# Attention scores of two heads at once on the two row halves of the array, six rounds instead of eleven steps, nine eviction buffers

## The chip, the cores and the metric

The kernel runs on one core of a Trainium2 chip, as one program. TensorE (PE, and PEld for its weight loads) multiplies, VectorE (DVE), ScalarE (ACT) and GpSimd (POOL) work on vectors, and SyncE (SP) issues the transfers from HBM. The metric is the device time of one execution in microseconds, less is better.

## The reference, cut to what matters

The program is two blocks of two layers each, on 256 tokens of width 1024, in float32. Each block has attention with 8 heads over the 256 tokens, causal and with a softmax over float32 scores. Block 1's mixer runs it beside a causal convolution over 31 tokens; block 2's mixer has three branches, of which A has 8 heads of 64 columns, B 4 heads with two score maps each, C 8 heads whose queries and keys are 64 + 32 columns.

```python
def mixer(u, cos, sin, ...):                      # block 1
    q, k, v, glu_in, g_attn, g_conv = jnp.split(u @ w_in, splits, axis=-1)
    attn = moba_attention(q, k, v)                # 8 heads of 64, causal at 256 tokens
    y_attn = attn @ w_attn_br
    y_conv = conformer_conv(glu_in, ...)          # depthwise, 31 taps, layer norm, silu, product
    merged = jax.nn.sigmoid(g_attn) * y_attn + jax.nn.sigmoid(g_conv) * y_conv
    return merged @ w_out
...
sc = jnp.einsum('brnqhc,brnkhc->brnhqk', qb, kw).astype(jnp.float32) * scale + bias   # branch A
p = probs(qa, k1) - lam * probs(qb, k2)                                               # branch B
sc = (einsum(qn, k_nope) + einsum(qr, k_rope)).astype(jnp.float32) * scale            # branch C
```

## The kernel before, in words

The main stream on PE is made of products with weights that stream in from HBM in pieces of 1 MB. Each piece is split into a high and a low part (ACT L138 writes `whi`, DVE L139 `wlo`), and `ws` (L160, L161, L164) multiplies both: 24 matmuls for one tile of 128 output columns. The attentions and the convolution are generators, "tracks", that advance beside this stream. `track(gen, steps, us)` registers one, and the stream calls `tick` after each `ws`, which takes as many steps as are due; `finish` takes all that are left, at once. So one step of an attention lies between two `ws`, and its position is fixed when the program is written.

`attend` has eleven steps. Step st issues the outputs of the pair of heads before (`matmul` L471 and L473, at odd steps from 3), the transposes of the probabilities of head st - 1 (`p_t`, three transposes at L450, then an ACT copy at L452), and the scores of head st (`probs`, L429 for the 128 queries of the first half, L430 for the others). Behind the scores DVE adds the bias and takes the negated row maximum (L433, L435), ACT takes the exponentials with row sums (L438, L439), DVE the reciprocal (L442), and `normalise` scales the numerators, the first 128 columns on ACT (L486), the others on DVE (L487). PE reads in the float32 form, which the trace shows as two instructions for each such matmul (one for each transpose). Everything that is copied out of PSUM or held for the softmax comes from the tag `ev`, 5 buffers of 2 KB a partition, used in turn.

A head of 64 columns fills 64 of the array's 128 rows: in block 1 and in branch A the heads 2i and 2i + 1 lie on the upper and the lower 64 partitions of the same tile (`qkf`). In branch C the operands are padded to 128 rows. Branch B (`diff`, L1328 to L1337) calls `probs` twice in a row, for its two maps on the two halves.

In block 1 the depthwise convolution is a track too (`conv`, L909 and L912 on DVE, 124 instructions in all). `mixer1` finishes the attention, then the convolution, and then transposes the convolution's result on PE (`conv_ln`, L927) for its layer norm. In the first layer other work on the small matmuls L408 and L418 lies between the `ws` as well, whose result DVE takes at L421.

Of the kernel before, what the change touches and what calls it, by code (L numbers as in the profile page):

```python
# [13 lines left out]
ALU = mybir.AluOpType  # L14
PSUM = bass.MemoryType.PSUM

P = 128
# [21 lines left out]
# columns of the packed per-partition parameters, and of the shape constants  # L39
# [21 lines left out]
PARTS = ((0, 512), (512, 768), (768, 1024))  # of the columns at the end of a product of 1024  # L61
# [3 lines left out]
class Net:  # L65
# [28 lines left out]
    def ev(self):  # L94
        return self.t("one", [P, 512], tag="ev", bufs=5)
# [6 lines left out]
    def track(self, gen, steps, us):  # L102
        """Advance gen by `steps` steps over the next `us` of the main stream."""
        t = [gen, steps / us, 0.0]
        self.tracks.append(t)
        return t
# [17 lines left out]
    def fetch(self, parts=1):  # L124
        """One packed piece of a weight: its float32 values as hi + lo, both float32r."""
# [16 lines left out]
    def w(self, ahead=2):  # L142
        """The next piece in weight_order; the pieces after it are already on their way."""
        while self.queue and len(self.ready) < 1 + ahead:
            self.fetch()
        return self.ready.pop(0)

    def split(self, hi, lo, src):
        """src (float32) as hi + lo."""
        a = self.nc.scalar.copy(hi, src)  # L150
        return a, self.nc.vector.tensor_sub(lo, src, hi.bitcast(F32))  # L151

    def ws(self, ps, w, blk, a, ks):
        """ps[cols of the weight, tokens] = W[:, cols]^T a   (weights stationary)."""
# [11 lines left out]
    def ws_pair(self, a, w=None):  # L166
        """Two column tiles (8 k tiles each) of the next weight piece -> psum [128, 2 x 256]."""
# [7 lines left out]
    def as_(self, ps, w, cols, a, k, h, first, last, **grp):  # L175
        """ps[tokens of half h, cols] += a^T W   (activations stationary)."""
# [64 lines left out]
    def rstd(self, v, w):  # L241
        """v (> 0, [128, w]) -> v ** -0.5: a guess from the exponent, two refinements."""
# [50 lines left out]
    def moments(self, st, eps, fill=()):  # L293
        """st: bn_stats of the pieces of a row -> mean, rstd."""
# [4 lines left out]
    def to_fm(self, src, n, evac):  # L299
        """src: [128 tokens, n * 128] in SBUF; evac(k0, nk, psum [128, nk, 128])."""  # L300
# [15 lines left out]
    def row(self, ap, n=D, pool="b4"):  # L316
        """A row of DRAM on all partitions."""
# [12 lines left out]
    def ada_cols(self, l, seg):  # L330
        """A shift (seg 0, 3) or 1 + scale (1, 4) as columns [128, 8]."""
# [8 lines left out]
    def ada_dot(self, l, seg, k, w):  # L340
        """One tile of columns: w [128 columns, 1024]; c_row is twice SiLU(c)."""
# [4 lines left out]
    def ada_work(self, segs):  # L346
        """On VectorE."""
# [32 lines left out]
    def ada_gate(self, l, seg, n, part, bb):  # L380
        """256 columns of a gate on all partitions: part summed over the partitions, + bias, + 1."""
# [10 lines left out]
    def ada_pe(self, segs):  # L392
        """On TensorE: 256 columns at a time, four k tiles side by side in the array."""
# [30 lines left out]
    def probs(self, q, k, bias):  # L424
        """q, k: [K, 256] feature-major (q scaled); bias [128, 256].  Unnormalised softmax numerators
        e [128, 384] (block 0: 128 keys | block 1: 256 keys) and the reciprocal row sums [128, 2]."""
        nc = self.nc
        p = self.ps()
        nc.tensor.matmul(p[:, 0:128], q[:, 0:128], k[:, 0:128], start=True, stop=True)  # L429
        nc.tensor.matmul(p[:, 128:384], q[:, 128:256], k, start=True, stop=True)  # L430
        e = self.ev()[:, :384]
        m = self.small(2, "att_m")
        nc.vector.tensor_tensor_reduce(e[:, 0:128], p[:, 0:128], bias[:, 128:256], -1.0, 3e38, ALU.add, ALU.min,  # L433
                                       m[:, 0:1])
        nc.vector.tensor_tensor_reduce(e[:, 128:384], p[:, 128:384], bias, -1.0, 3e38, ALU.add, ALU.min,  # L435
                                       m[:, 1:2])
        r = self.small(2, "att_r")
        nc.scalar.activation(e[:, 0:128], e[:, 0:128], AF.Exp, bias=m[:, 0:1], scale=-1.0, accum_out=r[:, 0:1])  # L438
        nc.scalar.activation(e[:, 128:384], e[:, 128:384], AF.Exp, bias=m[:, 1:2], scale=-1.0,  # L439
                             accum_out=r[:, 1:2])  # L440
        ri = self.small(2, "att_ri")
        nc.vector.reciprocal(ri, r)  # L442
        return e, ri

    def p_t(self, e):
        """e [128 queries, 384] -> [128 keys, 384]: keys 0 x 256 queries | keys 1 x queries of block 1."""
# [8 lines left out]
    def attend(self, qk, v, bias, y):  # L455
        """qk(h) -> q, k; v(h, j) -> [128 keys, 64]; y feature-major [128, 4, 256].  Each step: the scores of
        one head, the transposed probabilities of the one before, the output of the pair before that."""
        nc = self.nc
        es, pts, po = {}, {}, None
        for st in range(11):  # L460
            if st >= 3 and st % 2 == 1 or st == 10:
                pr = (st - 3) // 2
                if st < 10 and pr % 2 == 0:
                    po = self.ps()
                if st < 10:
                    for j in range(2):
                        for hh in range(2):
                            h = 2 * pr + hh
                            o = po[hh * 64:hh * 64 + 64, (pr % 2) * 256:(pr % 2) * 256 + 256]
                            if j == 0:  # L470
                                nc.tensor.matmul(o, v(h, 0), pts[h][:, 0:256], start=True, stop=False)  # L471
                            else:
                                nc.tensor.matmul(o[:, 128:256], v(h, 1), pts[h][:, 256:384], start=False, stop=True)  # L473
                    if pr % 2 == 1:
                        s = slice(pr - 1, pr + 1)
                        self.split(y[0][:, s, :], y[1][:, s, :], po.rearrange("p (k t) -> p k t", k=2))
            if 1 <= st <= 8:
                pts[st - 1] = self.p_t(es.pop(st - 1))
            if st < 8:
                e, ri = self.probs(*qk(st), bias(st))  # L480
                self.normalise(e, ri)
                es[st] = e
            yield

# [5 lines left out]
    def start(self):  # L490
        """Conditioning of the first mixer tile by tile, and with each tile its share of q, k, v and the
        first two pairs of the convolution's gated input."""
# [59 lines left out]
    def rel_bias(self):  # L552
        """DRAM [head, query in block, 256]: additive bias at distance 128 + p - j, -1e30 where masked."""
# [22 lines left out]
    def rope_tables(self):  # L576
        """cos, sin of positions * inv_freq for both halves: cc = [cos | cos], ss = [-sin | sin]."""
# [32 lines left out]
    def rope_tm(self, x, cc, ss):  # L610
        """In place: x [128, heads, 2, n]; cc, ss [128, 2, n]."""
# [50 lines left out]
    def later(self):  # L662
        """What is traced here issues behind the last handover."""
# [5 lines left out]
    class Norm:  # L669
        """x <- LN(ALPHA x + G acc) g + b;  u <- x A + B.   rms: x <- x + 0.5 acc;  u <- RMS norm of x times g.  # L670
        y: the rows before A, B (g)."""
# [12 lines left out]
        def transposed(self, h):  # L684
            """The row tiles k = 0, 1, 4, 5 in one bank, 2, 3, 6, 7 in another."""
# [931 lines left out]
```

## Time and profile before

| | |
|---|---|
| time, median of 3 runs | 1746.57 us (1746.49, 1746.57, 1747.38) |
| span of the profiled execution | 1744.7 us |
| median time less span | 1.87 us |
| PE busy | 1693.0 us, 97% |
| DVE busy | 1203.8 us, 69% |
| ACT busy | 894.8 us, 51% |
| PE waits for L912 at L927 | 5.1 us, once |

The profile gives no time of its own for the profiled execution apart from its span, so the span stands beside the median of the timed runs; what lies around it is the difference. A busy time is a sum over the whole span, in which stages with different limits follow each other. The attentions lie, in microseconds of the span, at 97 to 150 and 490 to 542 (block 1), 928 to 975 and 1400 to 1445 (branch A), 975 to 1022 and 1447 to 1492 (branch B), 880 to 924 and 1350 to 1395 (branch C).

### The profile page before, as it was taken

How to read it: one execution, taken by the hardware profiler on the slowest of the kernel's cores; microseconds unless marked ns; L12 is line 12 of the kernel's file. 1: busy time of each engine (PE TensorE's matmuls, PEld its weight loads, DVE VectorE, ACT ScalarE, POOL GpSimd, SP SyncE). 2: the span in 40 equal slices, each digit the busy share in tenths (PEclk: the TensorE clock that was granted, in tenths of full speed). 3: DMA queues.
4: the chain of work that ended last, by engine and by line, in shares of the span. 5: the costliest groups of instructions: out<-in, count | busy, mean ns of one | idle time of the engine just before them, and what ended most of it. 6: DMA issues, size and time to landing. Idle time of an engine off the chain costs nothing.

```text
span 1744.7 us, 28878 instructions
## 1 busy us (share of the span) xinstructions
PE 1693.0 (97%) x11736; PEld 1533.6 (88%) x11736; DVE 1203.8 (69%) x2281; ACT 894.8 (51%) x1550; POOL 2.6 (0%) x12
## 2 busy tenths in 40 slices
PE   6998999999999999988999999999999999999998
PEld 5887888888889899977998898999989889989997
DVE  7999887478997785468555667655675555875554
ACT  3664464355355455435566645444455666454442
POOL 0000000000000000000000000000000000000000
PEclk9999999999999999998999999999999999999999
DMA  9885568495865286635643344655454444446551
GB/s 339 339 309 188 190 228 332 168 341 187 300 233 206 97 320 217 205 130 207 209 140 130 138 156 137 239 190 191 151 210 161 147 145 145 163 158 209 183 184 47
DMA packets 59986, 347.58 MB, mean 199 GB/s; under 512 B 6558, under 2 KB 10700, under 8 KB 25676
## 3 DMA queue, kind: packets, MB, share of 16 engines
q1 hardware_dynamic: 59852, 345.73, 55.8%
q8 instruction: 92, 1.51, 0.3%
q14 instruction: 42, 0.34, 0.1%
HBM read 344.63 MB, written 2.64 MB: 199 GB/s over the span
## 4 chain that ended last, share of the span: by engine, by line
PE 89%; DVE 7%; ACT 2%; issue 1%; DMA 1%; SPq 0%; ACTq 0%; DVEq 0%
PE ps L160 16%; PE ps L161 16%; PE ps L164 16%; PE ps L181 8%; PE ps L180 8%; PE ps L182 7%; PE ps L196 3%; PE ps L202 3%; PE ps L197 3%; PE ps L430 1%; PE ps L450 1%; DVE wlo L139 1%; PE ps L306 1%; PE ps L429 1%; PE ps L408 1%
## 5 line engine op out<-in xcount | busy, mean ns | idle before, releaser
L139 DVE TENSOR_TENSOR wlo<-raw,whi 128x1024 fp32r<-128x1024 f32 (+1 forms) x534 | 630.4, 1212 | 306.1 <-ACT whi L138 304.2
L138 ACT CAST whi<-raw 128x1024 fp32r<-128x1024 f32 (+1 forms) x534 | 532.3, 1042 | 431.6 <-PE ps L161 186.2
L160 PE MATMUL ps<-s,whi 128*128 128x256 f32 x2400 | 602.6, 288 | 0.2 <-DVE s L901 0.2
L161 PE MATMUL ps<-s,whi 128*128 128x256 f32 x2400 | 590.5, 283 | 0.0
L160 PEld LDWEIGHTS ps<-s,whi 128*128 128x128 f32 x2400 | 459.8, 192 | 20.2 <-issue 16.1
L161 PEld LDWEIGHTS ps<-s,whi 128*128 128x128 f32 x2400 | 460.9, 192 | 2.4
L164 PE MATMUL ps<-s,wlo 128*128 128x256 f32 x2400 | 343.8, 284 | 1.3 <-DVE wlo L139 1.3
L164 PEld LDWEIGHTS ps<-s,wlo 128*128 128x128 f32 x2400 | 312.9, 192 | 1.5 <-DVE wlo L139 1.5
L180 PE MATMUL ps<-whi,s 128*128 128x512 f32 (+2 forms) x736 | 273.5, 372 | 12.8 <-ACT s L150 11.7
L181 PE MATMUL ps<-wlo,s 128*128 128x512 f32 (+2 forms) x736 | 273.1, 371 | 1.4 <-DVE wlo L139 1.4
L182 PE MATMUL ps<-whi,s 128*128 128x512 f32 (+2 forms) x736 | 271.8, 369 | 0.0
L180 PEld LDWEIGHTS ps<-whi,s 128*128 128x128 f32 x736 | 139.9, 190 | 34.7 <-ACT s L150 11.7
L181 PEld LDWEIGHTS ps<-wlo,s 128*128 128x128 f32 x736 | 139.9, 190 | 22.9 <-DVE wlo L139 2.5
L182 PEld LDWEIGHTS ps<-whi,s 128*128 128x128 f32 x736 | 139.6, 190 | 22.5
L196 PE MATMUL ps<-whi,s 128*128 128x512 f32 x240 | 97.9, 408 | 3.5 <-ACT s L761 3.5
L912 DVE SCALAR_TENSOR_TENSOR s<-s,dw,s 128x255 f32<-128x255 f32 (+14 forms) x240 | 96.8, 463 | 0.0
L197 PE MATMUL ps<-wlo,s 128*128 128x512 f32 x240 | 94.9, 396 | 0.0
L151 DVE TENSOR_TENSOR s<-ev,s 128x256 fp32r<-128x256 f32 (+1 forms) x72 | 39.1, 543 | 72.7 <-PE ps L181 54.0
L150 ACT CAST s<-ev 128x256 fp32r<-128x256 f32 (+1 forms) x72 | 36.1, 501 | 75.9 <-DVE ev L1392 73.5
L202 PE MATMUL ps<-whi,s 128*128 128x512 f32 x240 | 66.0, 398 | 0.0
L196 PEld LDWEIGHTS ps<-whi,s 128*128 128x128 f32 x240 | 45.8, 191 | 17.0 <-ACT s L761 5.4
L197 PEld LDWEIGHTS ps<-wlo,s 128*128 128x128 f32 x240 | 45.9, 191 | 9.1
(235 smaller groups left out, 1365.7 us busy)
## 6 DMA issues: line engine op xcount, KB each, us to landing
raw<-in_w_fgu_dram SPq DMA_DIRECT2D x44, 1024.0 KB, 4.9
raw<-in_w_up_dram SPq DMA_DIRECT2D x32, 1024.0 KB, 5.8
raw<-in_w_down_dram SPq DMA_DIRECT2D x32, 1024.0 KB, 5.1
raw<-in_w_in_dram SPq DMA_DIRECT2D x32, 1024.0 KB, 4.9
ada<-in_w_ada_p_dram SPq DMA_DIRECT2D x48, 512.0 KB, 4.6
raw<-in_w_gate_dram SPq DMA_DIRECT2D x24, 1024.0 KB, 4.8
raw<-in_w_fd_dram SPq DMA_DIRECT2D x22, 1024.0 KB, 4.8
raw<-in_w_in_b_dram SPq DMA_DIRECT2D x18, 1024.0 KB, 7.1
```

The source lines that it names most:

```text
L138: nc.scalar.copy(hi[:, a:b], raw[:, a:b])
L139: nc.vector.tensor_sub(lo[:, a:b], raw[:, a:b], hi[:, a:b].bitcast(F32))
L160: mm(ps, whi[:, b], ahi[:, k, :], start=j == 0, stop=False)
L161: mm(ps, whi[:, b], alo[:, k, :], start=False, stop=False)
L164: mm(ps, wlo[:, b], ahi[:, k, :], start=False, stop=j == n - 1)
L180: mm(ps, ahi[:, k, tok], whi[:, cols], start=first, stop=False, **grp)
L181: mm(ps, ahi[:, k, tok], wlo[:, cols], start=False, stop=False, **grp)
L182: mm(ps, alo[:, k, tok], whi[:, cols], start=False, stop=last, **grp)
L196: mm(p, ahi[:, k, tok], whi[:, cols], start=k == 0, stop=False)
L197: mm(p, ahi[:, k, tok], wlo[:, cols], start=False, stop=False)
L202: mm(p, alo[:, k, tok], whi[:, cols], start=False, stop=k == 7)
L912: nc.vector.scalar_tensor_tensor(cv[:, ct, d:], hp[:, ct, :S - d], wk, cv[:, ct, d:], op0=ALU.mult, op1=ALU.add)
```

## The change

`probs` takes a list of heads and issues the first 128 columns of scores for all of them, then the other 256, then the softmax head by head. `attend` runs in six rounds with ten steps: a round issues the outputs of pair rd - 2 and the scores of both heads of pair rd; after a `yield`, the transposes of both heads of pair rd - 1; and another `yield`. The tracks' step counts follow (11 to 10, and 23 to 22 for A and B together). `diff` hands its two maps to `probs` in one call. `ev` has nine buffers instead of five. The program is also built with a smaller scratch area for dynamic transfers, whose space the buffers take; all transfers here are on SP's queue. Comments are gone, so lines move by a few.

```diff
     def ev(self):
-        return self.t("one", [P, 512], tag="ev", bufs=5)
+        return self.t("one", [P, 512], tag="ev", bufs=9)
...
-    def probs(self, q, k, bias):
+    def probs(self, heads):
         nc = self.nc
-        p = self.ps()
-        nc.tensor.matmul(p[:, 0:128], q[:, 0:128], k[:, 0:128], start=True, stop=True)
-        nc.tensor.matmul(p[:, 128:384], q[:, 128:256], k, start=True, stop=True)
-        e = self.ev()[:, :384]
+        ps = [self.ps() for _ in heads]
+        for p, (q, k, _) in zip(ps, heads):
+            nc.tensor.matmul(p[:, 0:128], q[:, 0:128], k[:, 0:128], start=True, stop=True)
+        for p, (q, k, _) in zip(ps, heads):
+            nc.tensor.matmul(p[:, 128:384], q[:, 128:256], k, start=True, stop=True)
+        out = []
+        for p, (_, _, bias) in zip(ps, heads):
+            e = self.ev()[:, :384]
...
     def attend(self, qk, v, bias, y):
-        for st in range(11):
-            if st >= 3 and st % 2 == 1 or st == 10:
-                pr = (st - 3) // 2
...
-            if 1 <= st <= 8:
-                pts[st - 1] = self.p_t(es.pop(st - 1))
-            if st < 8:
-                e, ri = self.probs(*qk(st), bias(st))
-                self.normalise(e, ri)
-                es[st] = e
+        for rd in range(6):
+            if rd >= 2:
+                pr = rd - 2
...
+            if rd < 4:
+                hs = (2 * rd, 2 * rd + 1)
+                for h, (e, ri) in zip(hs, self.probs([(*qk(h), bias(h)) for h in hs])):
+                    self.normalise(e, ri)
+                    es[h] = e
             yield
+            if 1 <= rd <= 4:
+                for h in (2 * rd - 2, 2 * rd - 1):
+                    pts[h] = self.p_t(es.pop(h))
+                yield
...
-        att = self.track(self.attend(...), 11, 28.6)
+        att = self.track(self.attend(...), 10, 28.6)
-        ac = self.track(att_c(), 11, 30)
+        ac = self.track(att_c(), 10, 30)
-        ab = self.track(rest(), 23, 62)
+        ab = self.track(rest(), 22, 62)
...
-                pr = []
-                for j in range(2):
-                    r = slice(64 * j, 64 * j + 64)
-                    pr.append(self.probs(qb[r, st, :], kb[r, st, :], self.bias[2][:, st, :]))
-                (e1, r1), (e2, r2) = pr
+                rows = (slice(0, 64), slice(64, 128))
+                (e1, r1), (e2, r2) = self.probs([(qb[r, st, :], kb[r, st, :], self.bias[2][:, st, :]) for r in rows])
```

The first place is PE in branch A, first layer of block 2. Before, one step between two products (the L164 row ends the one ahead) has the outputs of a pair (L471, L473), the transposes of one head (L450) and the scores of another (L429, L430); `s` holds queries, keys and values, `ev` probabilities, `con` the identity matrix.

```order
L164 MATMUL ps_9507<-s_1118_7761,wlo_9328 128x256 x8
L471 MATMUL ps_9532<-ev_9437,s_1289_8751 64x256
L471 MATMUL ps_9532<-ev_9481,s_1289_8751 64x256
L473 MATMUL ps_9532<-ev_9437,s_1289_8751 64x128
L473 MATMUL ps_9532<-ev_9481,s_1289_8751 64x128
L450 MATMUL ps_9537<-con_116,ev_9486 128x128 x3
L429 MATMUL ps_9543<-s_1241_8405,s_1224_8244 128x128
L430 MATMUL ps_9543<-s_1241_8405,s_1224_8244 128x256
```

With the change, one step has the transposes of two heads (now L456), and the step one product later the outputs (L477, L479) and the scores of two heads (L431, L433).

```order
L164 MATMUL ps_9521<-s_1118_7761,wlo_9328 128x256 x8
L456 MATMUL ps_9603<-con_116,ev_9453 128x128 x3
L456 MATMUL ps_9609<-con_116,ev_9462 128x128 x3
...
L164 MATMUL ps_9625<-s_1118_7761,wlo_9417 128x256 x8
L477 MATMUL ps_9546<-ev_9607,s_1289_8751 64x256
L477 MATMUL ps_9546<-ev_9613,s_1289_8751 64x256
L479 MATMUL ps_9546<-ev_9607,s_1289_8751 64x128
L479 MATMUL ps_9546<-ev_9613,s_1289_8751 64x128
L431 MATMUL ps_9656<-s_1241_8405,s_1224_8244 128x128
L431 MATMUL ps_9657<-s_1241_8405,s_1224_8244 128x128
L433 MATMUL ps_9656<-s_1241_8405,s_1224_8244 128x256
L433 MATMUL ps_9657<-s_1241_8405,s_1224_8244 128x256
```

The scores of two heads have come together, and the transposes have moved away from them behind a product of their own.

The second place is PE at the end of block 1's attention, here in the second layer. Before, the last outputs follow a whole `ws` and two small matmuls behind the last transposes:

```order
L450 MATMUL ps_5449<-con_116,ev_5394 128x128 x3
...
L164 MATMUL ps_5414<-s_570_3923,wlo_5162 128x256 x8
L408 MATMUL ps_5479<-ada_5443,c_sel_487 32x256 x4
L408 MATMUL ps_5479<-ada_5445,c_sel_487 32x256 x4
L471 MATMUL ps_5380<-ev_5389,s_614_4177 64x256
L471 MATMUL ps_5380<-ev_5453,s_614_4177 64x256
L473 MATMUL ps_5380<-ev_5389,s_614_4177 64x128
L473 MATMUL ps_5380<-ev_5453,s_614_4177 64x128
L927 MATMUL ps_5563<-con_116,s_616_4179 128x128 x4
```

With the change `finish` takes the last two steps at the same place, and the outputs stand directly behind the transposes whose copies (`ev`, written by ACT) they read. L936 is the line of L927 now.

```order
L164 MATMUL ps_5403<-s_570_3923,wlo_5151 128x256 x8
L408 MATMUL ps_5467<-ada_5432,c_sel_487 32x256 x4
L408 MATMUL ps_5467<-ada_5434,c_sel_487 32x256 x4
L456 MATMUL ps_5482<-con_116,ev_5323 128x128 x3
L456 MATMUL ps_5488<-con_116,ev_5332 128x128 x3
L477 MATMUL ps_5438<-ev_5486,s_614_4177 64x256
L477 MATMUL ps_5438<-ev_5492,s_614_4177 64x256
L479 MATMUL ps_5438<-ev_5486,s_614_4177 64x128
L479 MATMUL ps_5438<-ev_5492,s_614_4177 64x128
L936 MATMUL ps_5563<-con_116,s_616_4179 128x128 x4
```

The product that lay between transposes and outputs has moved ahead of both; in the first layer the rows stand in the same way.

The third place is DVE in block 1's first layer, from the last head's scaling (L487) and the last L421 of this attention on. The rows left out are more steps of the convolution L912; L151 is the low part of the attention's last outputs.

```order
L487 TENSOR_SCALAR ev_1423<-ev_1423,att_ri_1430 128x256
L912 SCALAR_TENSOR_TENSOR s_60_497<-s_59_496,dw_498,s_60_497 128x240
L912 SCALAR_TENSOR_TENSOR s_60_497<-s_59_496,dw_498,s_60_497 128x239
L421 TENSOR_TENSOR ada_155_1087<-ps_1468,par_95 128x2
L912 SCALAR_TENSOR_TENSOR s_60_497<-s_59_496,dw_498,s_60_497 128x239
...
L151 TENSOR_TENSOR s_104_744<-ps_1409,s_103_743 128x512
```

With the change (L496 for the scaling, L921 for the convolution):

```order
L496 TENSOR_SCALAR ev_1361<-ev_1361,att_ri_1368 128x256
L921 SCALAR_TENSOR_TENSOR s_60_497<-s_59_496,dw_498,s_60_497 128x248
...
L421 TENSOR_TENSOR ada_153_1081<-ps_1457,par_95 128x2
L921 SCALAR_TENSOR_TENSOR s_60_497<-s_59_496,dw_498,s_60_497 128x242
...
L151 TENSOR_TENSOR s_104_744<-ps_1469,s_103_743 128x512
```

The last scaling has moved ahead of some 16 steps of the convolution, and L421 ahead of six: the convolution's two column tiles stand at width 242 there instead of 239, and the end is at 226 in both.

## Rows read from the trace of the kernel before

**Rows 1.** The page: busy time, share of the span and instructions of PE.

```profile
PE 1693.0 (97%) x11736; PEld 1533.6 (88%) x11736; DVE 1203.8 (69%) x2281; ACT 894.8 (51%) x1550; POOL 2.6 (0%) x12
```

**Rows 2.** Waits of PE over the whole span: total us, times, longest us.

```profile
PE ps L927 <- DVE s L912: 5.1, 1, 5.1
...
PE ps L450 <- ACT ev L486: 2.3, 3, 0.9
```

**Rows 3.** Windows: stretch, its length, busy us of each engine (instructions), clock, DMA.

```profile
97.00:150.00 53.00, 49.76 (x421) 40.77 (x420) 48.51 (x138) 32.59 (x74) 0.00 (x0) 1.00 0.69 254
490.00:542.00 52.00, 52.00 (x427) 43.18 (x424) 42.87 (x119) 30.45 (x72) 0.00 (x0) 1.00 0.59 209
...
928.00:975.00 47.00, 46.30 (x352) 40.36 (x351) 21.97 (x61) 30.58 (x74) 0.00 (x0) 1.00 0.43 148
975.00:1022.00 47.00, 46.80 (x390) 44.45 (x389) 30.90 (x91) 30.58 (x85) 0.00 (x0) 1.00 0.38 137
```

**Rows 4.** Timeline of PE, branch A, one head's scores: start, us, line, operation, operands.

```profile
930.39 0.49 PE L429 MATMUL ps<-s,s 64*128 64x128 f32 x2
...
931.24 0.39 PE L160 MATMUL ps<-s,whi 128*128 128x256 f32 x1
```

**Rows 5.** Timeline of PE, branch A: transposes, then scores.

```profile
934.22 0.49 PE L450 MATMUL ps<-con,ev 128*128 128x128 f32 x3
934.64 0.48 PE L429 MATMUL ps<-s,s 64*128 64x128 f32 x2
...
935.49 0.39 PE L160 MATMUL ps<-s,whi 128*128 128x256 f32 x1
```

**Rows 6.** Timeline of PE, branch A: outputs, transposes, scores.

```profile
942.78 0.65 PE L471 MATMUL ps<-ev,s 128*64 128x256 f32 x4
...
943.59 0.55 PE L450 MATMUL ps<-con,ev 128*128 128x128 f32 x3
944.06 0.48 PE L429 MATMUL ps<-s,s 64*128 64x128 f32 x2
...
944.91 0.39 PE L160 MATMUL ps<-s,whi 128*128 128x256 f32 x1
```

**Rows 7.** Timeline of PE, branch A: last transposes, and last outputs.

```profile
967.61 0.55 PE L450 MATMUL ps<-con,ev 128*128 128x128 f32 x3 [0.70 <-ACT ev L486]
967.91 0.37 PE L160 MATMUL ps<-s,whi 128*128 128x256 f32 x1
...
970.96 0.65 PE L471 MATMUL ps<-ev,s 128*64 128x256 f32 x4
...
971.76 0.39 PE L160 MATMUL ps<-s,whi 128*128 128x256 f32 x1
```

**Rows 8.** Timeline of PE, branch B: scores of two heads on two row halves.

```profile
977.70 0.50 PE L429 MATMUL ps<-s,s 64*128 64x128 f32 x4
...
978.57 0.39 PE L160 MATMUL ps<-s,whi 128*128 128x256 f32 x1
```

**Rows 9.** Timeline of ACT, branch A: start, us, line, operation, idle before.

```profile
935.92 0.41 ACT L438 ACTIVATE ev<-ev,att_m 128x128 f32<-128x128 f32 x1 [0.70 <-DVE att_m L433]
...
937.14 0.40 ACT L486 ACTIVATE ev<-ev,att_ri 128x128 f32<-128x128 f32 x1 [0.23 <-DVE att_ri L442]
...
944.17 0.48 ACT L452 COPY ev<-ps 128x384 f32<-128x384 f32 x1 [1.96 <-PE ps L450]
```

**Rows 10.** Chain of waits, end of block 1's first attention: start, us, what.

```profile
141.92 0.35 PE ps L418 x4
142.29 0.16 DVE ada L421
142.45 5.61 DVE s L912 x15
...
148.67 4.05 DVE s L912 x11
```

**Rows 11.** Window over the resumption behind that attention.

```profile
150.00:157.00 7.00, 4.24 (x19) 4.06 (x20) 7.00 (x17) 0.00 (x0) 0.00 (x0) 0.51 0.07 28
```

More of the change, by code (lines that the diff above doesn't have):

```diff
@@ L421, in ada_pe @@
                     nc.vector.tensor_add(self.ada_cols(l, seg)[:, k], p[:, 0:2], self.ada_bias(l, seg)[:, k])
-    def probs(self, q, k, bias):
+    def probs(self, heads):
         nc = self.nc
-        p = self.ps()
-        nc.tensor.matmul(p[:, 0:128], q[:, 0:128], k[:, 0:128], start=True, stop=True)
-        nc.tensor.matmul(p[:, 128:384], q[:, 128:256], k, start=True, stop=True)
-        e = self.ev()[:, :384]
[L432 to L443, printed above, removed]
+        ps = [self.ps() for _ in heads]
[6 more added lines that the diff above has]
+            e = self.ev()[:, :384]
+            m = self.small(2, "att_m")
+            nc.vector.tensor_tensor_reduce(e[:, 0:128], p[:, 0:128], bias[:, 128:256], -1.0, 3e38, ALU.add, ALU.min,
+                                           m[:, 0:1])
+            nc.vector.tensor_tensor_reduce(e[:, 128:384], p[:, 128:384], bias, -1.0, 3e38, ALU.add, ALU.min,
+                                           m[:, 1:2])
+            r = self.small(2, "att_r")
+            nc.scalar.activation(e[:, 0:128], e[:, 0:128], AF.Exp, bias=m[:, 0:1], scale=-1.0, accum_out=r[:, 0:1])
+            nc.scalar.activation(e[:, 128:384], e[:, 128:384], AF.Exp, bias=m[:, 1:2], scale=-1.0,
+                                 accum_out=r[:, 1:2])
+            ri = self.small(2, "att_ri")
+            nc.vector.reciprocal(ri, r)
+            out.append((e, ri))
+        return out
@@ L459, in attend @@
         es, pts, po = {}, {}, None
-        for st in range(11):
-            if st >= 3 and st % 2 == 1 or st == 10:
-                pr = (st - 3) // 2
-                if st < 10 and pr % 2 == 0:
+        for rd in range(6):
+            if rd >= 2:
+                pr = rd - 2
+                if pr % 2 == 0:
                     po = self.ps()
-                if st < 10:
-                    for j in range(2):
[L467 to L476, printed above, removed]
-            if 1 <= st <= 8:
-                pts[st - 1] = self.p_t(es.pop(st - 1))
-            if st < 8:
-                e, ri = self.probs(*qk(st), bias(st))
-                self.normalise(e, ri)
-                es[st] = e
@@ new lines, in attend @@
+                for j in range(2):
+                    for hh in range(2):
+                        h = 2 * pr + hh
+                        o = po[hh * 64:hh * 64 + 64, (pr % 2) * 256:(pr % 2) * 256 + 256]
+                        if j == 0:
+                            nc.tensor.matmul(o, v(h, 0), pts[h][:, 0:256], start=True, stop=False)
+                        else:
+                            nc.tensor.matmul(o[:, 128:256], v(h, 1), pts[h][:, 256:384], start=False, stop=True)
+                if pr % 2 == 1:
+                    s = slice(pr - 1, pr + 1)
+                    self.split(y[0][:, s, :], y[1][:, s, :], po.rearrange("p (k t) -> p k t", k=2))
@@ L1026, in mixer1 @@
         gates(0, [1])
-        att = self.track(self.attend(qkf, lambda h, j: v[:, j, 64 * h:64 * h + 64], lambda h: self.cmask, y), 11, 28.6)
+        att = self.track(self.attend(qkf, lambda h, j: v[:, j, 64 * h:64 * h + 64], lambda h: self.cmask, y), 10, 28.6)
         gates(0, [2, 3])
@@ L1333, in diff @@
             if st < 4:
-                pr = []
-                for j in range(2):
-                    r = slice(64 * j, 64 * j + 64)
-                    pr.append(self.probs(qb[r, st, :], kb[r, st, :], self.bias[2][:, st, :]))
-                (e1, r1), (e2, r2) = pr
+                rows = (slice(0, 64), slice(64, 128))
+                (e1, r1), (e2, r2) = self.probs([(qb[r, st, :], kb[r, st, :], self.bias[2][:, st, :]) for r in rows])
                 r2n = self.small(2, "r2n")
@@ L1605 @@
     from concourse.bass_utils import run_bass_kernel_spmd
-    nc = bacc.Bacc("TRN2", target_bir_lowering=False, num_devices=1)
+    nc = bacc.Bacc("TRN2", target_bir_lowering=False, num_devices=1, dynamic_dma_scratch_size=1024)
     arrays, aps = {}, {}
```

## The prediction

> **What bounds the kernel now.** The page's busy time comes first: PE is busy 1693.0 us of a span of 1744.7 us, 97%, and DVE only 69% [rows 1]. So an instruction taken off PE, or a gap closed on it, shows in the time, unless another engine is the limit in that stage. The view of PE's waits says where it is not PE: one wait of 5.1 us at L927, for the convolution's L912 on DVE, and three short ones at the transposes L450, 2.3 us together, for ACT's L486, which scales the probabilities [rows 2]. The windows by stage then show the stages that the change touches. In branch A (928 to 975) PE is busy 46.30 of 47 us and DVE 21.97; in block 1's second layer (490 to 542) PE has no idle at all and DVE 42.87 of 52; in block 1's first layer (97 to 150) DVE has 48.51 of 53, an idle time of 4.5 us, and that is the stage with the wait at L927 [rows 2, 3]. The second layer has no such wait.
>
> The timeline of PE prices the attention's pieces. I take each from its first matmul to the first of the next piece, which counts the change of shape with it. One head's scores: 930.39 to 931.24, .85 us [rows 4]. Transposes and one head's scores: 934.22 to 935.49, 1.27, of which the transposes .42 [rows 5]. Outputs of a pair, transposes, scores: 942.78 to 944.91, 2.13, in the parts .81, .47 and .85 [rows 6]. Transposes with products on both sides .30; outputs with products on both sides .80 [rows 7]. The row that matters most is in branch B, which already has its two score maps on two row halves: both together take 977.70 to 978.57, .87 us, as long as one head alone [rows 8]. The second head there is free, although B's program issues one map's matmuls after the other's.
>
> **The change, part by part.** No engine gets more or fewer operations; PE's matmuls come in other neighbourhoods.
>
> *One stage with row halves* (two layers of block 1, two of branch A). Before, it has one scores alone, four times transposes and scores, three times outputs, transposes and scores, one transposes alone, one outputs alone: .85 + 4 x 1.27 + 3 x 2.13 + .30 + .80 = 13.4 us [rows 4 to 7]. After, it has two pairs of scores alone, two outputs with a pair of scores behind, two outputs alone, and four times the transposes of two heads. A pair of scores is .87 [rows 8]. Outputs with scores directly behind are not in the trace: .81 + .85 = 1.66 is the floor, and transposes between these two cost .47 instead of the .30 between products, so a change between such shapes may cost .17, ceiling 1.83; I take 1.75, the middle. Six transposes in a row are not in it either: between twice .30 and twice .47; I take .66, near the floor, since products stand on both sides as in rows 7. The sum is 2 x .87 + 2 x 1.75 + 2 x .80 + 4 x .66 = 9.5 us; the saving 3.9, with the bounds 2.7 and 4.4.
>
> *Branch A.* The saving is whole, because DVE has 25 us idle in it [rows 3] and ACT 16. The wait of .70 at the last transposes [rows 7] also goes: it was for a scaling only one step old, and the transposes now come at least two steps behind their scores. 3.9 + .7 = 4.6 in each layer, 9.2 for both; bounds 6.8 and 10.2.
>
> *Block 1, second layer.* The last step now issues transposes and, directly behind them, the outputs that need both their copies (the order shown with the change). In branch A the copy behind transposes that start at 943.59 runs from 944.17 for .48 [rows 6, 9]: 1.06 us after their start, a second copy 1.54. PE is done with the six transposes after .66. So it waits .9, with the last semaphore 1.0; between .4 (if only the first copy counted) and 2.1 (if one head's exponentials, 935.92 to 937.14, 1.22 us, stand ahead of the copies on ACT). The convolution is not late here, as the missing wait shows. 3.9 - 1.0 = 2.9; bounds .6 and 4.0.
>
> *Block 1, first layer.* Here the end is not PE's. The chain of waits runs on PE up to the small product L418 at 141.92, goes over to DVE's L421, and then stays in 26 convolution steps of L912 until 152.7 [rows 10]; PE waits for that. Up to that L418 PE has .85 + 4 x 1.27 + 3 x 2.13 and a wait of .9 [rows 2], 13.2 us, and will have 2 x .87 + 2 x 1.75 + 3 x .66 = 7.2: DVE is released 6 us earlier. But six more convolution steps then stand behind L421 (33 up to the convolution's end instead of 27, counted in the program's order), 6 x .37 us by rows 10 (9.66 us for 26), 2.2: at most 3.8 earlier. DVE's own idle time, 4.5 us, is a second ceiling [rows 3]. New idle time comes in where DVE's two reciprocals of a pair wait for two heads' exponentials, 1.22 us a head on ACT [rows 9]. I take 3.0, near the ceiling, and for the range 0 to 3.8. The wait at L927 gets longer all the same, since PE arrives earlier than it is released.
>
> *Branch C* issues its heads in pairs too, but its scores use all 128 rows, so nothing overlaps: 0, within 1 us either way. *Branch B* keeps its instructions and already overlaps [rows 8]: 0. The four buffers more keep both heads' numerators and copies alive; without them the pair's second head would wait for a copy. They cost SBUF only. SP issues the same transfers but for one small one.
>
> The sum is 9.2 + 2.9 + 3.0 = 15.1 us. The profiled execution has a span of 1744.7 us; the median of the three times is 1746.57, 1.9 above it, which I leave as it is. 1746.57 - 15.1 = 1731.5 us.
>
> **The rivals.** *DVE keeps the first layer* (18 in 100). The two heads' row maxima come together, the convolution steps pile up behind them, and the end at 152.7 stays where it is: 12.1 us, 1734.5. For it: 48.51 of 53 us busy [rows 3] and the chain [rows 10]. Against it: that chain starts from PE, not from DVE. A longer wait may also hold TensorE's clock down longer: behind the wait of before the granted clock is .51 from 150 to 157, the lower of its two levels, and PE resumes at 152.7 within it [rows 10, 11]. If it stays there for as long again, 4.3 us at half speed cost 2.1, and the time is 1736.6.
>
> The Trainium skill, page "TensorEngine Tiling (Array Packing)", Performance Considerations, PSUM Bottleneck, says of this that tiling speeds up TensorE but not the emptying of PSUM, which may become the limit. The trace agrees for the first layer and not for branch A, where DVE is busy 47% of the window [rows 3]; by the rule held for every stage the gain would shrink to nothing, by the rows it is lost in one stage of four, which is the 1734.5 above.
>
> *The halves do not overlap here* (5 in 100): a pair costs 1.70, not .87. That takes 4 x .83 = 3.3 from each stage, leaving .6; A has 2 x 1.3, the second layer loses .4, the first gains nothing: 2.2 us, 1744.4. Against it stands row after row of B.
>
> *The softmax of two heads comes too late* (7 in 100, the other side). If in each of the 20 rounds outside the first layer the transposes wait for the second head's exponentials, 1.22 us [rows 9], and the old waits of 1.4 us stay, the time is 1746.57 - 13.7 + 24.4 = 1757.3. It decides from 15.1 / 20 = .76 us a round. Against it: from one head's scores at 934.64 to the start of its scaling at 937.14 are 2.5 us [rows 5, 9], with .40 for it and 1.22 for the second head 4.1; the transposes come two or three steps later, and a step is 930.39 to 934.22, 3.8 us [rows 4, 5].
>
> **How the numbers follow.** My forecast has 70 in 100, with 1727.6 to 1740 as the extremes if all bounds went one way; its own range is 1728 to 1735. The first rival spans 1734.5 to 1736.6. I give 1727 to 1738, which leaves out the second and third rivals and some of the tails. A measurement of this kernel tells 0.2%, 3.5 us, from no change. The forecast and the first rival are faster (88), the second the same (5), the third slower (7).
>
> **What would show it.** In A, two heads' scores from start to the next product .87, six transposes near .66, no wait at the transposes, and the stage's window shorter by some 4.6 us. In block 1's second layer a new wait of about 1 us at the last outputs, for ACT's copy. In its first layer the wait at the convolution's transposes at about 6 us instead of 5.1, ending about 3 us earlier (PE comes there 13.4 + .9 - 9.5 - 1.0 = 3.8 us earlier); if it ends at the same time, the first rival holds. Waits at the transposes in every round would make the prediction wrong, and so would a pair of scores at 1.7.

## The result and the profile after

The changed kernel takes 1728.51 us (median of 4, 1728.24 to 1731.38), the kernel before 1746.97 us in the same comparison: ratio 0.9895, 95% interval 0.9881 to 0.9909, that is 18.5 us faster by the medians. The forecast was 1731.5. Run again later the changed kernel took 1729.37 us beside 1747.04 us, 17.7 less. One execution of the version below with the scaling on ACT took 2053 us, at a granted clock of .75, and is left out of its median.

The profiled execution has a span of 1729.6 us, 15.1 under that of before. A span can be followed through the program by the start of the same matmul of the main stream in both traces; the lead of the changed kernel, by stage:

| stretch, us of the span before | start before, after | lead behind it | gained in it |
|---|---|---|---|
| start of the program, to 94 | 94.08, 96.06 | -1.98 | -1.98 |
| block 1, first layer, to 154 | 154.10, 152.58 | 1.52 | 3.50 |
| to 488 | 488.04, 486.45 | 1.59 | .07 |
| block 1, second layer, to 541 | 541.07, 536.57 | 4.50 | 2.91 |
| to 870 | 870.05, 867.48 | 2.58 | -1.92 |
| branch C, to 926 | 926.10, 923.30 | 2.80 | .22 |
| branch A, to 972 | 971.76, 963.65 | 8.11 | 5.31 |
| branch B, to 1013 | 1013.06, 1004.27 | 8.79 | .68 |
| to 1345 | 1345.21, 1336.37 | 8.85 | .06 |
| branch C, to 1397 | 1397.05, 1387.98 | 9.07 | .22 |
| branch A, to 1443 | 1443.07, 1428.69 | 14.38 | 5.31 |
| branch B, to 1485 | 1485.08, 1470.02 | 15.06 | .68 |
| to the end | 1730.11, 1715.05 | 15.05 | 0 |

The eight stages with an attention gain 18.8 us. The start and the stretch from 541 to 870 lose 3.9 in this execution. In the profile of the changed kernel run again, the start loses 1.2 instead of 2.0, the stretch from 541 to 870 .2 instead of 1.9, and the one from 154 to 488 .9 instead of nothing, while each of the eight stages gains the same within .01: those losses change from one execution to the next, and the gain of the stages does not.

The waits of PE over the whole span (total us, times, longest us), which answer to [rows 2]:

```profile
PE ps L936 <- DVE s L921: 5.8, 1, 5.8
...
PE ps L477 <- ACT ev L458: 0.9, 2, 0.5
```

The transposes have no wait left. L477, the outputs, has two new ones of .46, one in each layer of block 1; and the wait for the convolution is .7 us longer than before.

The timeline of PE in branch A, first layer (start, us, line, operands), against [rows 4 to 8]:

```profile
927.59 0.49 PE L431 MATMUL ps<-s,s 64*128 64x128 f32 x4
...
928.45 0.39 PE L160 MATMUL ps<-s,whi 128*128 128x256 f32 x1
...
935.34 0.82 PE L456 MATMUL ps<-con,ev 128*128 128x128 f32 x6
935.92 0.36 PE L160 MATMUL ps<-s,whi 128*128 128x256 f32 x1
...
938.96 0.65 PE L477 MATMUL ps<-ev,s 128*64 128x256 f32 x4
...
939.76 0.49 PE L431 MATMUL ps<-s,s 64*128 64x128 f32 x4
...
940.62 0.39 PE L160 MATMUL ps<-s,whi 128*128 128x256 f32 x1
```

Two heads' scores take .86 from start to the next product, as the two maps of branch B did. The six transposes of two heads take .58; outputs with the scores of two heads behind them take 1.66, .80 + .86. A stage that was 13.4 us is now 2 x .86 + 2 x 1.66 + 2 x .80 + 4 x .58 = 9.0.

The timeline of PE at the end of block 1's second layer:

```profile
532.02 0.87 PE L456 MATMUL ps<-con,ev 128*128 128x128 f32 x6
533.35 0.81 PE L477 MATMUL ps<-ev,s 128*64 128x256 f32 x3 [0.46 <-ACT ev L458]
533.84 0.38 PE L479 MATMUL ps<-ev,s 128*64 128x128 f32 x2
534.00 0.38 PE L477 MATMUL ps<-ev,s 128*64 128x256 f32 x1
534.22 0.38 PE L479 MATMUL ps<-ev,s 128*64 128x128 f32 x2
534.53 1.09 PE L936 MATMUL ps<-con,s 128*128 128x128 f32 x8
535.38 0.37 PE L160 MATMUL ps<-s,whi 128*128 128x256 f32 x1
```

and that of ACT at the same place:

```profile
532.07 0.59 ACT L1026 ACTIVATE s<-ps 128x512 f32<-128x512 f32 x1
532.56 0.36 ACT L411 COPY ev<-ps 128x256 f32<-128x256 f32 x1
532.81 0.87 ACT L458 COPY ev<-ps 128x384 f32<-128x384 f32 x2
```

PE starts the first outputs 1.33 us after the first transposes, where six transposes alone take .58: .75 late. The timeline calls .46 of it a wait for the copies L458; the first of these stands behind L1026 (.59) and L411 (.36) in ACT's queue. The outputs then run in two pieces, and take 533.35 to 534.53, 1.18 instead of .80.

### The profile page after: what moved, and what is told of

It reads as the page before. It is cut to its first block, busy times and chain, and to the rows that moved or that the text cites. A ratio compares the mean times of both kernels' runs of the same rounds, so it can differ in the third digit from the quotient of the medians.

```text
span 1729.6 us, 28838 instructions
## 1 busy us (share of the span) xinstructions
PE 1676.8 (97%) x11736; PEld 1526.7 (88%) x11736; DVE 1203.0 (70%) x2281; ACT 886.2 (51%) x1550; POOL 2.6 (0%) x12
## 4 chain that ended last, share of the span: by engine, by line
PE 88%; DVE 7%; DMA 2%; ACT 2%; issue 1%; SPq 0%; ACTq 0%; DVEq 0%
PE ps L160 16%; PE ps L161 16%; PE ps L164 16%; PE ps L181 7%; PE ps L180 7%; PE ps L182 7%; PE ps L196 3%; PE ps L202 3%; PE ps L197 3%; DVE wlo L139 1%; PE ps L306 1%; PE ps L408 1%; PE ps L456 1%; PE ps L433 1%; DMA raw<-in_w_in_a_dram 1%
## 5 line engine op out<-in xcount | busy, mean ns | idle before, releaser
L139 DVE TENSOR_TENSOR wlo<-raw,whi 128x1024 fp32r<-128x1024 f32 (+1 forms) x534 | 630.1, 1212 | 332.4 <-ACT whi L138 331.8
L164 PE MATMUL ps<-s,wlo 128*128 128x256 f32 x2400 | 343.7, 283 | 1.3 <-DVE wlo L139 1.3
L164 PEld LDWEIGHTS ps<-s,wlo 128*128 128x128 f32 x2400 | 312.8, 192 | 1.5 <-DVE wlo L139 1.5
L921 DVE SCALAR_TENSOR_TENSOR s<-s,dw,s 128x255 f32<-128x255 f32 (+14 forms) x240 | 96.4, 463 | 0.0
L151 DVE TENSOR_TENSOR s<-ev,s 128x256 fp32r<-128x256 f32 (+1 forms) x72 | 39.1, 543 | 73.4 <-PE ps L181 55.8
```

The source lines that it names most:

```text
L139: nc.vector.tensor_sub(lo[:, a:b], raw[:, a:b], hi[:, a:b].bitcast(F32))
L164: mm(ps, wlo[:, b], ahi[:, k, :], start=False, stop=j == n - 1)
L921: nc.vector.scalar_tensor_tensor(cv[:, ct, d:], hp[:, ct, :S - d], wk, cv[:, ct, d:], op0=ALU.mult, op1=ALU.add)
```

## The experiments

Each kernel is the changed one with one edit, if nothing else is said.

**Same rows.** Does the gain come from the row halves?

```diff
-                r = slice(64 * (h % 2), 64 * (h % 2) + 64)
+                r = slice(0, 64)
```

> The changed kernel, but the heads of block 1 and of branch A all read their queries and keys from the lower 64 partitions (the odd heads so use the wrong operands); order, counts and buffers stay. Theory one, overlap: two heads' scores cost .87 us only because they lie on different row halves; on one half a pair costs about 1.7, so each of the four pairs in a stage costs .84 more. In both layers of A and in block 1's second layer that is 3 x 3.4 = 10 us, in block 1's first layer 0 to 1, because PE waits for the convolution there: 1728.5 + 10 = 1738 to 1740. Theory two, grouping: the gain comes from fewer changes of shape and from waits that went: within 1 us of 1728.5.

Measured: 1740.29 us, ratio 0.9957 (0.9943 to 0.9972): 10.9 to 11.8 us slower than the changed kernel in its two runs. Theory one holds. The timeline of PE in branch A:

```profile
928.91 0.71 PE L431 MATMUL ps<-s,s 64*128 64x128 f32 x4
929.46 1.03 PE L433 MATMUL ps<-s,s 64*128 64x256 f32 x4
930.41 0.39 PE L160 MATMUL ps<-s,whi 128*128 128x256 f32 x1
```

A pair on one half takes 1.50 us against .86, so the overlap is worth .64 a pair, 2.6 a stage, not the .84 expected: two heads issued as neighbours on one half (1.50) are already cheaper than two apart (2 x .85). Four stages of 2.6 make 10.4, about what was measured, so the first layer of block 1 lost its share as well, though the theory gave it 0 to 1: its gain by the leads is .87 instead of 3.50. Why is seen below. Theory two falls only as the whole cause: without the overlap the eight stages still gain 8.3 of the 18.8 us by the leads, so the row halves are worth some 10.5 and the new order the rest.

**Head by head.** Does the alternating order matter?

```diff
         for p, (q, k, _) in zip(ps, heads):
             nc.tensor.matmul(p[:, 0:128], q[:, 0:128], k[:, 0:128], start=True, stop=True)
-        for p, (q, k, _) in zip(ps, heads):
             nc.tensor.matmul(p[:, 128:384], q[:, 128:256], k, start=True, stop=True)
```

> The changed kernel with the two heads' scores issued head by head (128 and 256 columns of the first head, then of the second) instead of alternating. If the array itself overlaps neighbours on other rows, as branch B of the kernel before seems to show: within 1 us of 1728.5. If matmuls overlap only with the one directly ahead in the program: one of the two matmuls of a pair is no longer covered, some .3 to .5 us per pair, 4 to 6 us over the three stages on PE's path, 1733 to 1735.

Measured: 1729.28 us, ratio 0.9901 (0.9884 to 0.9917), no difference that can be told. The timeline of PE in branch A shows the same .86, with the narrow matmuls (L431) of both heads ahead of the wide ones although the built program has them head by head:

```profile
924.80 0.50 PE L431 MATMUL ps<-s,s 64*128 64x128 f32 x4
925.13 0.61 PE L432 MATMUL ps<-s,s 64*128 64x256 f32 x4
925.66 0.38 PE L160 MATMUL ps<-s,whi 128*128 128x256 f32 x1
```

**Five buffers.**

```diff
-        return self.t("one", [P, 512], tag="ev", bufs=9)
+        return self.t("one", [P, 512], tag="ev", bufs=5)
```

> The changed kernel with five eviction buffers as before, instead of nine. Used in turn, the second head's numerators then take the buffer of the first head of the pair before, which its transposes read only one product later, so DVE waits some 3 us in each of four rounds a stage. Theory, buffers matter where DVE decides: 5 to 14 us slower, most of it in block 1's first layer, that is 1733 to 1743. Rival, buffers do not matter (PE is ahead of nobody who is late): within 1 us of 1728.5.

Measured: 1730.0 us, ratio 0.9897 (0.9883 to 0.9912). The median is 1.5 us above the 1728.5 of the rival and .6 above the second time of the changed kernel; the profile decides for the rival: each of the eight stages gains the same as with nine buffers, and the wait at L936 is 5.8 us in both. The four buffers are not needed.

**Nine buffers in the kernel before** (with the smaller scratch area).

> The kernel before with nine eviction buffers and the smaller scratch area alone. Theory: no buffer is late in the kernel before, the three waits at the transposes are for ACT's queue: within 1 us of 1746.6. Rival: the buffers remove those waits: 2.3 us less, about 1744.

Measured: 1747.86 us, ratio 1.0002 (0.9992 to 1.0011). Nothing, as the theory has it: buffers and scratch area are no part of the gain.

**Earlier attention in block 1.** The last outputs get their product between them and the transposes back.

```diff
-        att = self.track(self.attend(qkf, ..., lambda h: self.cmask, y), 10, 28.6)
+        att = self.track(self.attend(qkf, ..., lambda h: self.cmask, y), 10, 26.0)
```

> The changed kernel with block 1's attention spread over 26.0 us of the stream instead of 28.6, so that its last outputs come one product behind the last transposes again instead of directly behind them. Theory: the waits of .9 us for ACT's copies go in both layers; in the second layer PE's path gets about 1 us shorter, in the first layer the end is still the convolution's and DVE is released at most one product earlier: 1 to 2 us faster than the changed kernel, 1726.5 to 1727.5. Rival: the copies are covered elsewhere and the wait moves to the convolution: within .5 us of 1728.5.

Measured: 1726.79 us, ratio 0.9881 (0.9867 to 0.9896), and run again (below) 1727.14. In the timeline of PE, second layer, the outputs come 4.6 us behind the transposes and in one piece, .80 long:

```profile
526.51 0.82 PE L456 MATMUL ps<-con,ev 128*128 128x128 f32 x6
...
531.13 0.65 PE L477 MATMUL ps<-ev,s 128*64 128x256 f32 x4
531.61 0.39 PE L479 MATMUL ps<-ev,s 128*64 128x128 f32 x4
531.93 1.09 PE L936 MATMUL ps<-con,s 128*128 128x128 f32 x8
```

The second layer gains 4.41 us over the kernel before (lead 3.21 at 488, 7.62 at 541) instead of 2.91, 1.5 more where about 1 was expected: the new wait of the changed kernel costs 1.5 there. The first layer gains 3.57 instead of 3.50: there the wait at L936 has grown to 7.0 us, so PE comes earlier and is not let go earlier.

**Fewer taps.** Is the convolution the end of the first layer?

```diff
-        for d in range(CK):
+        for d in range(CK - 6 if l == 0 and pair == 1 else CK):
```

> The changed kernel without the last 6 taps of the second pair of the convolution in the first layer, 12 instructions of DVE of about .37 us (so the first layer's convolution lacks them). Theory, DVE's convolution sets the end of that stage: the wait of 5.8 us at the convolution's transposes shrinks by 4.4 and the time with it, 1724. Rival, the wait only names DVE and PE is held by its own path or by the half clock behind it: within 1 us of 1728.5.

Measured: 1722.95 us, ratio 0.9860 (0.9846 to 0.9875): 5.6 to 6.4 us faster than the changed kernel in its two runs. The wait at L936 is down from 5.8 to 1.4 us, the 4.4 expected. Most of the rest comes with the clock: these are the windows from 147 to 180 (length, busy us of PE, PEld, DVE, ACT, POOL, then the granted clock), first of the changed kernel, then of this one.

```profile
147.00:180.00 33.00, 28.76 (x237) 26.22 (x238) 30.64 (x72) 11.93 (x20) 0.00 (x0) 0.90 0.62 217
```

```profile
147.00:180.00 33.00, 32.45 (x284) 29.88 (x283) 30.36 (x66) 15.13 (x24) 0.00 (x0) 1.00 0.77 272
```

Behind the long wait the mean granted clock is .90 of 2.4 GHz; behind the short one it is never reduced. Counted from the start of the stage, the matmuls of this version are 4.4 us ahead of the changed kernel's by the wait alone and 6.1 us ahead by 149, where those of the changed kernel run at half clock; a new wait of .5 us, for DVE at the transposes L306, is most of what brings that back to 5.3 by 159.

**B at its old rate.**

```diff
-        ab = self.track(rest(), 22, 62)
+        ab = self.track(rest(), 22, 59.2)
```

> The changed kernel with the steps of A and B spread over 59.2 us instead of 62, the rate of the kernel before. Theory: branch B gained .7 us in each layer because its first transposes now stand two products behind their scores instead of one, and this gain goes back: 1.3 us slower, 1729.8. Rival: it gained because both maps' scores are issued together: within .5 us of 1728.5.

Measured: 1732.67 us, ratio 0.9920 (0.9903 to 0.9936), 3.3 to 4.2 slower than the changed kernel. The theory has the sign and the place, and half of the size by the leads. The first transposes of branch B in the timeline of PE, of the kernel before, the changed kernel and this one:

```profile
981.84 0.83 PE L450 MATMUL ps<-con,ev 128*128 128x128 f32 x3
982.60 0.50 PE L429 MATMUL ps<-s,s 64*128 64x128 f32 x4
```

```profile
973.42 0.49 PE L456 MATMUL ps<-con,ev 128*128 128x128 f32 x3
973.84 0.49 PE L431 MATMUL ps<-s,s 64*128 64x128 f32 x4
```

```profile
968.69 0.74 PE L456 MATMUL ps<-con,ev 128*128 128x128 f32 x3 [0.92 <-DVE ev L1349]
969.36 0.49 PE L431 MATMUL ps<-s,s 64*128 64x128 f32 x4
```

Before, three transposes take .76 to the scores, after .42. At the old rate they take .67, and .92 of idle time for DVE's L1349, which combines the two maps, stands ahead of them: both branches lose 1.3 us by the leads, 2.7 together. Measured from the start of the matmul ahead of each, the transposes of the kernel before come .6 us late in all, the first two as DVE's two instructions of that line (L1343 there) end at 981.78 and 982.18; with the change none is late, and at the old rate they come 1.3 late. So nothing shows a gain of branch B from issuing both maps together: at the old rate the changed form is .65 slower than the kernel before in each layer.

**Products into the wait.** In the first layer half of the attention's branch product goes ahead of the convolution's transposes.

```diff
+        if first:
+            branch(0, y, 0, None)
         self.finish(conv)
...
-        branch(0, y, 0, None)
+        branch(0, y, 1 if first else 0, None)
         next(cl)
-        branch(0, y, 1, None)
+        if not first:
+            branch(0, y, 1, None)
```

> The changed kernel where block 1's first layer multiplies the first half of the attention branch before the convolution's transposes instead of behind them. Theory, PE waits there only because nothing else stands ahead of the convolution: about 6 us of products fill the wait of 5.8, of which the last outputs' split on DVE, 14 convolution steps ahead of the end, may leave a part: 4 to 5.5 us faster, 1723 to 1724.5, more if the half clock behind the wait goes too (2 us). Rival: the evacuation of these products queues on DVE behind the convolution and the wait comes back in the second product: within 1 us of 1728.5.

Measured: 1730.3 us, ratio 0.9904 (0.9889 to 0.9919): no faster than the changed kernel (1728.51 and 1729.37). The rival holds in the time; of its mechanism, the wait that comes back is for ACT as well as for DVE. The waits of PE from 140 to 185 us (total us, times, longest us):

```profile
PE ps L936 <- DVE s L921: 2.0, 1, 2.0
PE ps L387 <- ACT ev L411: 1.9, 1, 1.9
PE ps L161 <- DVE s L151: 1.4, 2, 1.0
PE ps L160 <- ACT s L150: 0.8, 1, 0.8
```

The single wait of 5.8 us has become 6.1 us at four lines, for DVE and for ACT: DVE is busy 29.49 of the 33 us from 147 to 180 in this run, 30.64 in the changed kernel (the window shown above), and filling this hole on PE only moved the wait.

**Scaling on ACT** in the first layer, on top of the earlier attention, the first time beside that version and the changed kernel, the second time alone.

```diff
     def normalise(self, e, ri):
         self.nc.scalar.mul(e[:, 0:128], e[:, 0:128], ri[:, 0:1])
-        self.nc.vector.tensor_scalar(e[:, 128:384], e[:, 128:384], ri[:, 1:2], None, op0=ALU.mult)
+        if self.act_norm:
+            self.nc.scalar.mul(e[:, 128:384], e[:, 128:384], ri[:, 1:2])
+        else:
+            self.nc.vector.tensor_scalar(e[:, 128:384], e[:, 128:384], ri[:, 1:2], None, op0=ALU.mult)
```

> The version with the attention of block 1 spread over 26.0 us, and in block 1's first layer both parts of the probabilities scaled on ACT: eight instructions of .35 us leave DVE, which has 1.4 us of idle time in that stage, and eight of about .5 go to ACT, which has 21. Theory, DVE's sum of work sets the end of the first layer: 2.8 us faster than that version, about 1724. Rival, ACT's longer queue delays the reciprocals' operands and the copies, so that DVE or PE idles instead: within 1 us of that version.

> The version with the attention of block 1 spread over 26.0 us once more, beside the changed kernel in the same chip job. Theory: the second layer's wait for ACT's copies is gone, and what hangs on it behind: 1.5 to 3 us faster than the changed kernel. Rival: its time before was scatter of the start of the program: within .5 us of it.

> The changed kernel once more, as the measure for the two others of this job: 1728 to 1730. A profiled execution whose first 50 us are 2 us shorter than in the one seen first would show that those 2 us are not the change's.

Measured: 1727.26 us with the scaling on ACT, ratio 0.9885 (0.9871 to 0.9900); 1727.14 for the earlier attention alone, 0.9882 (0.9865 to 0.9898); 1729.37 for the changed kernel, 0.9898 (0.9883 to 0.9913). The earlier attention is 2.2 us under the changed kernel, as theory has it. The scaling shows no difference in the time, but its profile does in the stage: the wait of PE at the convolution (L941 there) is 4.8 us instead of 7.0, and between the matmuls at 88.75 and 154.78 of the version without it the first layer gains 2.7 us. The same execution lost 3.0 us ahead of 88.75, where the programs are equal. So it was run once more.

> The version with the scaling on ACT once more. Its first profile had 2 to 3 us more in the first 88 us, before any attention, and 2.7 us less in block 1's first layer. If the slow start was scatter of that execution: the first 88 us are like the others here and the time is 2 to 3 us under the version with 26.0 us alone, about 1724.5. If it belongs to the kernel: the start is again 2 us longer, and the time again about 1727.

Measured: 1726.29 us (median of three), ratio 0.9875 (0.9855 to 0.9894). The start is like the others now (the matmul at 88.75 us in the version without is at 88.86), and the first layer is 2.3 us shorter, by the leads. The time is .5 to .9 under that of the earlier attention, less than its scatter: the 2 to 3 us stand in the stage in both profiles. Part of them is lost at the end: in both profiles the last transfer of the output lands .9 us later behind the last product, whose first matmul then stands 15.4 us ahead of the end of the span; in every other profile it is 14.5 to 14.6. Why is open, and so is how much of the rest stands in the time.

## Why the prediction was right

The range and the likeliest case hold: faster, by the mechanism that was priced, at 1728.5 for 1731.5. The stages gained 18.8 us for 15.1, and no term came out below its forecast; the time lies 1.5 us from the lower bound of the range of 1727. By its steps:

**Price of a stage.** 9.5 us were forecast and 9.0 came out. The scores of two heads (.87, now .86) were read right from branch B; six transposes are .58 instead of .66, and outputs with scores behind them 1.66, the floor of the range and not the middle taken: a direct change between these shapes costs nothing extra. Of the saving of 4.5 the overlap proper is 2.6, as the run on one half shows; .8 is that two heads' scores stand together (1.50 for 1.70, four times), and 1.1 that the transposes stand between products (4 x .58 for 4 x .42 + 3 x .47 + .30).

**Branch A.** 5.31 in each layer for 4.6: .5 from these prices, and the vanished wait was worth about the rest, 5.31 - 4.46 = .85, more than the .70 that the views give it. This step is the largest term that was mis-sized, by 1.4 us in both layers.

**Block 1, second layer.** 2.91 for 2.9, and that it agrees so well is luck. The new wait stands where it was put, .75 late and .38 for the outputs in two pieces in the timeline, but the run with the earlier attention takes it away and gains 1.5: the wait cost 1.5 for the 1.0 forecast, and the saving of the stage was 4.5 for 3.9. The two errors cancel.

**Block 1, first layer.** 3.50 for 3.0, and the wait at the convolution 5.8 for the 6 forecast. But the step's reason was not whole. It put DVE's release at L421; the chain of waits of the changed kernel goes another way (start, us, what):

```profile
143.38 0.39 ACT ev L458
143.81 0.76 PE ps L477 x3
...
145.09 0.59 ACT s L150
145.71 0.69 DVE s L151
146.40 4.79 DVE s L921 x13
151.24 1.69 PE ps L936 x6
```

PE's last outputs, .46 late for the copies, then ACT's and DVE's split of them, and only then 13 of the convolution's steps: DVE stands idle .67 us ahead of L151, for ACT's half of that split. The chain of the run on one half ends in the same pieces, 2.6 us later counted from the start of the stage: that is why that run lost its 2.6 us here too, against what its theory said. So 3.50 lies near 3.0 by another last wait than the one the prediction named. The windows of the first layer (length, busy us of PE, PEld, DVE, ACT, POOL, clock), of the changed kernel, of the run on one half, and of the earlier attention, with the longer window of the kernel before:

```profile
97.00:150.00 53.00, 47.97 (x446) 40.63 (x435) 51.59 (x147) 32.23 (x76) 0.00 (x0) 0.99 0.71 261
```

```profile
97.00:150.00 53.00, 48.87 (x423) 41.77 (x422) 49.14 (x141) 31.42 (x74) 0.00 (x0) 0.99 0.71 258
```

```profile
97.00:150.00 53.00, 45.97 (x427) 39.40 (x425) 51.33 (x149) 31.57 (x74) 0.00 (x0) 0.97 0.69 259
```

```profile
147.00:180.00 33.00, 27.92 (x232) 24.97 (x229) 30.55 (x73) 12.70 (x23) 0.00 (x0) 0.90 0.68 229
```

DVE's idle time in 53 us is 4.5 before [rows 3], 1.4 after, 3.9 on one half and 1.7 with the earlier attention: it is the gap that PE's saving closes, 3.1 us by the first two, and with the gap closed the earlier attention, whose last outputs come a product sooner, brought .07 more. So the first rival, DVE keeps the layer, was wrong for this change, and it came true in that further one. The page "TensorEngine Tiling (Array Packing)" of the Trainium skill, Performance Considerations, PSUM Bottleneck, has it that the emptying of PSUM may become the limit behind faster matmuls. Where the prediction says that the trace agrees for the first layer, it reads too much into the busy share: DVE is full there, 51.6 of 53 us, but of its work from 97 to 152 us the convolution L921 is 33.3 us and the split of the weights L139 13.3, neither of which reads PSUM, and the four lines that empty PSUM (L438, L440, L151, L421) are 7.8. So the rows do not show that the emptying of PSUM is the limit here.

The clock was not held down longer by the longer wait, as the first rival's dearer case had it: from 147 to 180 the mean granted clock is .90 in both kernels (the window of the changed kernel stands with the fewer taps).

**Branch C, branch B.** C was given 0 within 1 us and gained .22 in each layer, which no run here explains. B was given 0 and gained .68 in each. That is a term that the prediction missed: it looked at B's instructions and not at the rate of the track that steps them. With 22 steps over 62 us instead of 23, two products instead of one stand between the first scores and their transposes, and DVE's combination is in time. The run at the old rate gives it back, and .65 more in each layer.

**The other rivals.** The halves overlap (.86 a pair). The softmax of two heads is in time: the transposes wait nowhere, with nine buffers or with five. What the prediction says of the buffers, that without them the second head would wait for a copy, is wrong; five are enough.

**Own time and span.** The forecast set the stages' sum, 15.1 us, against the median; the stages gave 18.8 and the medians 18.5 and 17.7.

## What to carry to other kernels

Where a matmul fills half of the array's rows, price the pair from a place where the program already runs two on two halves; here that one row gave the price to .01 us, and the program's order within the pair made no difference. Count the rate at which steps are taken as part of a change: two terms, the wait at the end of block 1 and the gain of branch B, came from a step count that looked like bookkeeping. Before a hole on one engine is filled, look at the sum of work of the engine that it waits for: here filling the wait of 5.8 us with products gained nothing, and taking 4.4 us off DVE gained 5.6.

The version that beats both kernels clearly is the changed one with block 1's attention over 26.0 us: 1726.8 and 1727.1 us in its two runs, about 2 under the changed kernel; none of its eight executions is as slow as the fastest of the changed kernel's eight.

## What the runs showed of the hardware that was not expected

PE did not keep the program's order between matmuls on different row halves: issued head by head, both narrow matmuls started ahead of both wide ones in the trace (924.80 and 925.13), at the same .86 us. A pair on one half cost 1.50, less than twice one head's .85. A removed wait was worth more than its length: with 4.4 us less of it the granted clock stayed at full speed, and the kernel gained 5.6.
